# Thirteen feature units of the mixers as split products, their parts made on ScalarE and GpSimd

## The chip, the core and the metric

The kernel runs on one core of one Trainium2 chip. Five engines work side by side, each through its own list of instructions in order: TensorE (PE) multiplies, VectorE (DVE), ScalarE (ACT) and GpSimd (POOL) do the elementwise work, and SyncE (SP) issues most of the loads from device memory. They wait for one another by semaphores. The metric is the device time of the whole program in microseconds, lower is better.

## The reference

Two layers of a decoder trunk on 256 tokens of width 1024, all in float32. A layer is a half-step SwiGLU FFN (inner width 2816), a hybrid token mixer and a second FFN, each behind an RMS norm that a conditioning vector `c` shifts, scales and gates:

```python
mod = (cond @ ada_w[l] + ada_b[l]).reshape(B, N_SUBLAYERS, 3, 1, D)
h = adaln_pre(x, norm_g[l, 1], mod[:, 1, 0], mod[:, 1, 1])
p = dict(zip(names, jnp.split(h @ w_in[l] + b_in[l], splits, axis=-1)))
y_a = nsa_mixer(p["a_q"], ...)           # sparse attention
y_b = short_conv_mixer(p["b_b"], p["b_c"], p["b_x"], sc_conv_w[l])
y_c = gated_deltanet(p["c_q"], ..., p["c_z"], ...)   # chunked delta rule, triangular solve
y_d = mlstm_mixer(p["d_q"], p["d_k"], ..., p["d_o"], ...)
y = jnp.concatenate([rms_norm(y_a, ...), rms_norm(y_b, ...), y_c, y_d], axis=-1)
x = x + mod[:, 1, 2] * (y @ w_out[l])
```

The columns of `w_in` are cut into units of 128 features: `k0 k1 q0 q1 v0 v1` and `z0 z1` of the delta rule, `dq0 dq1 dk0 dk1 o0 o1` of the mLSTM, `b0 b1 c0 c1 x0 x1` of the short convolution, `aq0 aq1 ksw kvc` of the attention.

## The kernel before

Activations stand with features on the 128 partitions and the 256 tokens along them, so `h` is eight blocks of 128 × 256. A unit is a weight of 128 × 1024 and a sum over eight k-steps, one block of `h` each. There are two ways to multiply. A float32 product (`mm`) is one call and two instructions on PE. A split product (`mm3`, line 262) uses two float32r parts of each operand, the rounded value `h` and the rest `l`, and sums three products, hi·hi, hi·lo and lo·hi. `split_into` makes the parts: ACT casts, another engine subtracts. The FFNs use split products; the units of the mixer use float32 products on the whole weight and on `hF`, the float32 `h`.

In the mixer PE, DVE, ACT and POOL are switched to a written order (`InOrder`): each engine issues in the order of the source, and SP's loads go out in the order of the source too. The source is one long list, in which `step(name, n)` gives PE n k-steps of a unit, between the small products of the four head groups. Buffers come from rings of tags: `raw` has four, `wh`, `wl`, `bg` and `bx` three each. `load(tag)` takes the next unit of the list `units` and issues its load into a buffer of that tag; `used(name)`, called behind the last k-step of a unit, frees its tag and loads the next unit. While the mixer runs, `CAP` lets units use `wh` and `wl` and keeps `raw` for the adaLN weights: `ada_load` loads 128 outputs of `ada_w`, and `ada_use` is one DVE product of 128 × 1024, `aw`, with an accumulated sum.

Names that return below, in the order in which PE meets them. `lf` (DVE, from the token-major unit `td`) goes into `bc`, the cumulative sums. `glh` and `gll` are the parts of the log gates; POOL multiplies them with a triangle of `cst` into `ug`, four tiles a layer, from which PE makes the gates' differences `sg` and `sgx`. `ssc` and `rsk` are norms. `kq` and `kr` are products of the delta rule's keys and queries that DVE scales into `AP`. `MV`, `wh` and `hid` belong to the attention's compression. `nMh` and `nMl` are the parts of the mLSTM's running maxima, from which PE makes `mw`. `As`, `T`, `Q`, `Tt` and `Ab` belong to a blockwise inversion of two triangular matrices, numbered 0 and 1; POOL copies `Ab` from `As`, and PE's `q` reads it. `taps(n, u)` is a causal convolution of four taps on DVE (`cvk`, `cvq`, `cvv`), one `TENSOR_SCALAR` and three `SCALAR_TENSOR_TENSOR`. At the end the output projection takes eight units `wo`.

## Time and profile before

| | us |
|---|---|
| median of three runs | 1207.26 (1205.89 to 1207.42) |
| profiled execution | 1206.86 |
| span of its trace | 1205.1 |
| PE busy | 1176.2 (98%) |
| DVE busy | 811.3 (67%) |
| ACT busy | 473.6 (39%) |
| POOL busy | 276.6 (23%) |
| mixer of layer 0 | 228 to 424 |
| mixer of layer 1 | 810 to 1007 |

The span is what the profiler saw of one execution; the time also holds 1.8 us around it. The granted clock of PE stands at 9 tenths or more in each of the page's 40 slices. An engine's busy time counts its instructions, not its waits. In a timeline an instruction's row ends with the idle time ahead of it and with what ended that, and instructions of one kind that follow each other are one row with a count.

### The profile page before, as it was taken

What the parts mean: (1) busy time and instruction counts of PE and PEld (TensorE: products, weight loads), DVE (VectorE), ACT (ScalarE), POOL (GpSimd) and SP (SyncE); (2) the same over time, 40 slices, a digit from 0 to 9 for tenths busy, and PEclk for the clock granted to TensorE, in tenths of its full rate; (3) what the DMA queues carried; (4) which work ended last, traced back from release to release, by engine and by line L of the source; (5) the groups of instructions that cost most, each with busy time, mean ns of one, the idle gap of its engine ahead of it and who ended that gap; (6) DMA issues with size and microseconds to landing.
All of it is one profiled execution on the core that took longest, in us unless ns stands there. A gap on an engine that the chain in (4) does not pass through costs nothing.

```text
span 1205.1 us, 21205 instructions
## 1 busy us (share of the span) xinstructions
PE 1176.2 (98%) x8402; PEld 1088.6 (90%) x8402; DVE 811.3 (67%) x1536; ACT 473.6 (39%) x829; POOL 276.6 (23%) x233
## 2 busy tenths in 40 slices
PE   5999999999999999999999999999999999999998
PEld 4799999978769889999999999998776998999998
DVE  4667887258967568888647777734697774766663
ACT  3454454222222255444435444433122334544441
POOL 0022432202010033434231333220201002332321
PEclk9999999999999999999999999999999999999999
DMA  8988896466574337989756787664656442676561
GB/s 282 320 326 306 318 353 214 162 211 213 176 273 158 117 104 268 318 305 310 232 179 203 251 280 274 203 226 174 211 166 244 165 144 71 210 244 227 176 193 53
DMA packets 77748, 266.96 MB, mean 222 GB/s; under 512 B 8815, under 2 KB 14191, under 8 KB 77505
## 3 DMA queue, kind: packets, MB, share of 16 engines
q1 hardware_dynamic: 68256, 232.00, 56.1%
q0 software_dynamic: 8960, 32.88, 8.3%
q8 instruction: 66, 1.08, 0.4%
q10 hardware_dynamic: 432, 0.72, 0.2%
q14 instruction: 34, 0.28, 0.1%
HBM read 264.50 MB, written 2.24 MB: 221 GB/s over the span
## 4 chain that ended last, share of the span: by engine, by line
PE 89%; DVE 7%; DMA 2%; ACT 1%; issue 1%; ACTq 0%; SPq 0%; DVEq 0%
PE ab L198 35%; PE y L198 21%; PE e L198 8%; PE po L198 2%; PE p_td L198 2%; PE pw L198 2%; DVE aw L198 2%; PE hid L198 1%; PE p_o L198 1%; PE p_dk L198 1%; PE p_z L198 1%; PE p_aq L198 1%; PE p_x L198 1%; PE pv L198 1%; PE tq L198 1%; PE p_b L198 1%
## 5 line engine op out<-in xcount | busy, mean ns | idle before, releaser
L198 PE MATMUL y<-g,w_2h 128*128 128x256 f32 x1408 | 257.1, 284 | 0.0
L198 POOL TENSOR_TENSOR w_2l<-w,w_2h 128x1024 fp32r<-128x1024 f32 x71 | 174.7, 2461 | 355.3 <-ACT w_2h L198 314.7
L198 DVE SCALAR_TENSOR_TENSOR aw<-aw,cond 128x1024 f32<-128x1024 f32 x144 | 246.9, 1715 | 13.3 <-DMA aw<-in_adaw_dram 8.0
L198 PEld LDWEIGHTS y<-g,w_2h 128*128 128x128 f32 x1408 | 219.3, 192 | 0.9 <-issue 0.9
L198 PE MATMUL y<-g,w_2l 128*128 128x256 f32 x704 | 199.9, 284 | 0.0
L198 PE MATMUL ab<-hH,w_0h 128*128 128x256 f32 x600 | 168.9, 281 | 1.3 <-DVE sl L198 1.3
L198 PE MATMUL ab<-hH,w_1l 128*128 128x256 f32 x600 | 167.8, 280 | 1.3 <-DVE w_1l L198 1.3
L198 PE MATMUL ab<-hH,w_1h 128*128 128x256 f32 x600 | 168.2, 280 | 0.0
L198 PE MATMUL ab<-hH,w_0l 128*128 128x256 f32 x600 | 167.7, 280 | 0.0
L198 PE MATMUL ab<-hL,w_0h 128*128 128x256 f32 x600 | 167.6, 279 | 0.0
L198 PE MATMUL ab<-hL,w_1h 128*128 128x256 f32 x600 | 167.6, 279 | 0.0
L198 DVE TENSOR_TENSOR w_1l<-w,w_1h 128x1024 fp32r<-128x1024 f32 x75 | 102.7, 1369 | 57.1 <-ACT w_1h L198 56.2
L198 PEld LDWEIGHTS y<-g,w_2l 128*128 128x128 f32 x704 | 134.7, 191 | 0.0
L198 ACT CAST w_2h<-w 128x1024 fp32r<-128x1024 f32 x88 | 91.8, 1047 | 107.5 <-PE ab L198 96.7
L198 ACT CAST w_1h<-w 128x1024 fp32r<-128x1024 f32 x75 | 78.7, 1049 | 115.0 <-PE ab L198 97.9
L198 PEld LDWEIGHTS ab<-hH,w_0h 128*128 128x128 f32 x600 | 113.0, 188 | 2.1 <-issue 2.1
L198 PEld LDWEIGHTS ab<-hH,w_1l 128*128 128x128 f32 x600 | 113.0, 188 | 1.5 <-DVE w_1l L198 1.5
L198 PEld LDWEIGHTS ab<-hH,w_0l 128*128 128x128 f32 x600 | 113.0, 188 | 0.2 <-DVE w_0l L198 0.2
L198 PEld LDWEIGHTS ab<-hL,w_0h 128*128 128x128 f32 x600 | 112.8, 188 | 0.0
L198 PEld LDWEIGHTS ab<-hH,w_1h 128*128 128x128 f32 x600 | 112.7, 188 | 0.0
L198 PEld LDWEIGHTS ab<-hL,w_1h 128*128 128x128 f32 x600 | 112.4, 187 | 0.0
L198 DVE TENSOR_TENSOR sl<-sl,ab 128x256 f32<-128x256 f32 x75 | 31.5, 420 | 107.3 <-ACT sl L198 107.3
(442 smaller groups left out, 1898.8 us busy)
## 6 DMA issues: line engine op xcount, KB each, us to landing
w<-in_ffn_dram SPq DMA_DIRECT2D x238, 512.0 KB, 4.5
aw<-in_adaw_dram SPq DMA_DIRECT2D x88, 512.0 KB, 4.9
aw<-in_adaw_dram POOLq DMA_DIRECT2D x56, 512.0 KB, 5.2
we<-in_ffn_dram SPq DMA_DIRECT2D x18, 512.0 KB, 4.1
wh<-in_cw_dram SPq DMA_DIRECT2D x16, 512.0 KB, 3.6
wwo<-in_wout_dram SPq DMA_DIRECT2D x16, 512.0 KB, 3.6
we<-in_ffn_dram SPq DMA_DIRECT2D x32, 128.0 KB, 4.8
wtd<-in_wtd_dram SPq DMA_DIRECT2D x8, 412.0 KB, 4.8
```

Of the source, the lines that this page charges most:

```text
L198: r = f(*args, **kw)
```

## The change

Thirteen of the fourteen units `dq`, `b`, `c`, `x`, `dk`, `o`, `z` of each mixer become split products; b1 stays a float32 product. For each of them `ahead()`, called behind the third k-step of a running unit, takes two free buffers and issues a cast on ACT (`w…h`) and a subtraction on POOL (`w…l`), for at most two units in advance; the weight's own buffer is then free for the next load. `both(k)` makes the parts `hH` and `hL` of a block of `h`, on ACT and DVE, for four blocks between td1 and td2 and for four in front of the taps of k0. A load may now take any free buffer of `wl`, `raw` or `wh`. One load of adaLN weights of each mixer moves into the FFN ahead of it, and the whole FFN weights that are loaded early get a memset of one column or an order behind another instruction.

```diff
+        split_units = [n for n in units if n[:-1] in ("dq", "b", "c", "x", "dk", "o", "z")]
+        ready, live, firsts = {}, {}, {}
+        CAP = {"raw": 4, "wh": 3, "wl": 3, "bg": 1, "bx": 1}
+        def free(tag):
+            return CAP[tag] - list(live.values()).count(tag)
         def used(n):
-            tag = live.pop(n)
-            if units and not (tag in ("bg", "bx") or list(live.values()).count(tag) >= CAP[tag]):
-                load(tag)
+            if n in firsts:
+                live.pop(n + "h")
+                live.pop(n + "l")
+                firsts.pop(n)
+            else:
+                live.pop(n)
+            more()
+        def space():
+            return sum(max(free(t), 0) for t in ("wl", "wh", "raw"))
+        def slot():
+            return next(t for t in ("wl", "raw", "wh") if free(t) > 0)
+        def more():
+            while units and space() > (2 if split_units and len(firsts) < 2 else 0):
+                load(slot())
+        def ahead():
+            if split_units and split_units[0] in ready and len(firsts) < 2 and space() > 1:
+                n = split_units.pop(0)
+                r, both = ready[n], []
+                for c in "hl":
+                    tag = live[n + c] = slot()
+                    both.append(wk.tile([128, 1024], F32R, tag=tag, bufs=BUFS[tag], name=f"w{n}{c}"))
+                firsts[n] = ready[n] = both
+                act.copy(both[0], r)
+                pool.tensor_tensor(both[1], r, both[0].bitcast(F32), op=ALU.subtract)
+                live.pop(n)
+                more()
+        def both(k):
+            act.copy(hH[:, k], hf32(k)[:, :T])
+            dve.tensor_tensor(hL[:, k], hf32(k)[:, :T], hH[:, k].bitcast(F32), op=ALU.subtract)
@@ dense
+            if name in split_units:
+                split_units.remove(name)
                 for k in range(KD):
-                    mm(hf(p, u), w[:, 128 * k:128 * k + 128], hf32(k)[:, :T], start=(k == 0), stop=(k == KD - 1))
+                    if isinstance(w, list):
+                        mm3(hf(p, u), w, hT, (ALL, slice(128 * k, 128 * k + 128)), (ALL, k), k == 0, k == KD - 1)
+                    else:
+                        mm(hf(p, u), w[:, 128 * k:128 * k + 128], hf32(k)[:, :T], start=(k == 0), stop=(k == KD - 1))
+                    if k == 2:
+                        ahead()
@@ mixer
-        CAP["raw"] = 0
+        CAP["raw"] = 1
         step("aq1")
         placed_on_all("aq")
         ada_load(sync, "raw")
-        ada_load(sync, "raw")
...
         step("td1", 3)
+        for k in range(4):
+            both(k)
         step("td2")
...
         tanh_of("q")
+        for k in range(4, KD):
+            both(k)
         step("kvc", 2)
         taps("k", 0)
@@ calls
-        a1.run(28 if l == 0 else 20, first=(l == 0))
+        a1.run(29 if l == 0 else 21, first=(l == 0))
```

The order on POOL in the first mixer, from the first `ug` to the first copies `Ab`. Before:

```order
L198 TENSOR_TENSOR ug_2816<-cst,glh 128x512
L198 TENSOR_TENSOR ug_2818<-cst,gll 128x512
L198 MEMSET gpv 128x2x3
L198 TENSOR_TENSOR ug_2858<-cst,glh 128x512
L198 TENSOR_TENSOR ug_2860<-cst,gll 128x512
L198 MEMSET MV 128x32x16
L198 COPY Ab_3081<-As_3011 128x256
L198 COPY Ab_3135<-As_3037 128x256
```

And now, from the third subtraction on:

```order
L198 TENSOR_TENSOR wb0l<-wb_2683,wb0h 128x1024
L198 TENSOR_TENSOR ug_2883<-cst,glh 128x512
L198 TENSOR_TENSOR ug_2885<-cst,gll 128x512
L198 MEMSET gpv 128x2x3
L198 TENSOR_TENSOR wc0l<-wc_2768,wc0h 128x1024
L198 TENSOR_TENSOR ug_2937<-cst,glh 128x512
L198 TENSOR_TENSOR ug_2939<-cst,gll 128x512
L198 TENSOR_TENSOR wc1l<-wc_2822,wc1h 128x1024
L198 MEMSET MV 128x32x16
L198 TENSOR_TENSOR wx0l<-wx_2896,wx0h 128x1024
L198 TENSOR_TENSOR wx1l<-wx_2898,wx1h 128x1024
L198 TENSOR_TENSOR wdk0l<-wdk_3144,wdk0h 128x1024
```

```order
L198 TENSOR_TENSOR wdk0l<-wdk_3144,wdk0h 128x1024
L198 TENSOR_TENSOR wdk1l<-wdk_3177,wdk1h 128x1024
L198 COPY Ab_3244<-As_3128 128x256
L198 COPY Ab_3298<-As_3190 128x256
L198 COPY Ab_3376<-As_3190 128x256
```

`wc0l` stands ahead of the second pair of `ug`, which goes into `sgx`, and all subtractions up to `wdk1l` stand ahead of the first `Ab`.

The order on DVE ahead of `lf`, from the bias of the second half of the token-major values (`dvaug`) to the small tiles of the gates (`lt`). Before:

```order
L198 TENSOR_TENSOR dvaug<-p_td_2644,par_657 128x4x64
L198 SCALAR_TENSOR_TENSOR aw_46_2654,mod<-aw_46_2654,cond 128x1024
L198 TENSOR_SCALAR cvk<-gpk,par_657 128x256
L198 SCALAR_TENSOR_TENSOR cvk<-gpk,par_657,cvk 128x256 x3
L198 SCALAR_TENSOR_TENSOR aw_47_2679,mod<-aw_47_2679,cond 128x1024
L198 TENSOR_TENSOR modG<-mod,par_70 128x8
L198 TENSOR_SCALAR lt<-ex 128x16
```

And now:

```order
L198 TENSOR_TENSOR dvaug<-p_td_2643,par_657 128x4x64
L198 SCALAR_TENSOR_TENSOR aw_47_2686,mod<-aw_47_2686,cond 128x1024
L198 TENSOR_TENSOR modG<-mod,par_70 128x8
L198 TENSOR_TENSOR hL<-hF_2391,hH 128x256 x4
L198 TENSOR_SCALAR cvk<-gpk,par_657 128x256
L198 SCALAR_TENSOR_TENSOR cvk<-gpk,par_657,cvk 128x256 x3
L198 SCALAR_TENSOR_TENSOR aw_48_2714,mod<-aw_48_2714,cond 128x1024
L198 TENSOR_SCALAR lt<-ex 128x16
```

Four `hL` now stand between the two products `aw`, ahead of the taps; `lf` follows the gates' tiles in both.

The order on SP around the loads of wdk0 and wdk1, whose buffers come free as the text above says. Before:

```order
L253 DMA wx1_2803<-in_winf_dram 128x1024
L253 DMA wh0_2823<-in_cw1_dram 128x1024
L358 DMA aw0_55_3008<-in_adaw_dram 128x1024
L253 DMA wh1_2900<-in_cw1_dram 128x1024
L253 DMA wdk0_2957<-in_winf_dram 128x1024
L358 DMA aw0_56_3025<-in_adaw_dram 128x1024
L253 DMA wdk1_3005<-in_winf_dram 128x1024
```

And now:

```order
L253 DMA wx1_2898<-in_winf_dram 128x1024
L358 DMA aw0_54_3057<-in_adaw_dram 128x1024
L358 DMA aw0_55_3125<-in_adaw_dram 128x1024
L253 DMA wh0_3008<-in_cw1_dram 128x1024
L253 DMA wh1_3073<-in_cw1_dram 128x1024
L358 DMA aw0_56_3162<-in_adaw_dram 128x1024
L253 DMA wdk0_3144<-in_winf_dram 128x1024
L253 DMA wdk1_3177<-in_winf_dram 128x1024
```

The two loads of dk now follow each other; wdk0 goes into the buffer that `wx1l` releases on POOL and wdk1 into that of wdk0, released by `wdk0l`, where before the last k-step of a unit on PE released it.

## Rows read from the trace of the kernel before

**Rows 1.** Part 1 of the page.

```profile
PE 1176.2 (98%) x8402; PEld 1088.6 (90%) x8402; DVE 811.3 (67%) x1536; ACT 473.6 (39%) x829; POOL 276.6 (23%) x233
```

**Rows 2.** Windows: length, busy PE, PEld, DVE, ACT, POOL, clock, DMA share, GB/s.

```profile
228.00:424.00 196.00, 193.89 (x1100) 158.22 (x1099) 131.26 (x396) 56.02 (x146) 22.23 (x33) 1.00 0.53 178
810.00:1007.00 197.00, 195.09 (x1107) 159.35 (x1106) 132.03 (x396) 57.30 (x149) 22.70 (x33) 1.00 0.52 176
290.00:310.00 20.00, 19.33 (x101) 14.62 (x100) 17.23 (x51) 4.84 (x11) 0.55 (x1) 1.00 0.42 141
310.00:330.00 20.00, 19.60 (x121) 14.54 (x120) 17.73 (x44) 5.54 (x14) 1.81 (x4) 1.00 0.56 185
330.00:350.00 20.00, 20.00 (x126) 12.74 (x124) 13.63 (x37) 5.72 (x16) 2.58 (x5) 1.00 0.78 268
```

**Rows 3.** Timeline of PE: start, length, what, count, idle before and its releaser.

```profile
277.92 0.39 PE L198 MATMUL bc<-lf,cst 128*128 128x8 f32 x2 [0.51 <-DVE lf L198]
...
289.27 0.82 PE L198 MATMUL sg<-ug,cstR 128*128 128x512 f32 x2
...
290.59 0.63 PE L198 MATMUL sgx<-ug,onesR 128*128 128x512 f32 x2
...
307.17 6.22 PE L198 MATMUL p_x<-hF,wx 128*128 128x256 f32 x28
...
317.86 0.32 PE L198 MATMUL mw<-nMl,cstR 4*128 4x128 f32 x1 [0.40 <-DVE nMl L198]
...
320.24 0.61 PE L198 MATMUL q<-T,Ab 128*128 128x128 f32 x4
```

**Rows 4.** Timeline of DVE, same columns.

```profile
276.78 1.01 DVE L198 TENSOR_SCALAR ob<-ex 128x32 f32<-128x32 f32 x1
277.71 0.16 DVE L198 TENSOR_SCALAR lf<-sp 128x8 f32<-128x8 f32 x1
...
292.05 0.17 DVE L198 TENSOR_SCALAR xk<-ssc 128x8 f32<-128x8 f32 x1 [3.98 <-PE ssc L198]
...
309.31 1.22 DVE L198 SCALAR_TENSOR_TENSOR aw<-aw,cond 128x1024 f32<-128x1024 f32 x1
...
317.40 0.40 DVE L198 TENSOR_TENSOR nMl<-negM,nMh 4x256 fp32r<-4x256 f32 x1
```

**Rows 5.** Chain of waits: start, length, what.

```profile
69.61 5.66 PE ab L198 x48
...
249.47 6.92 PE p_aq L198 x32
```

**Rows 6.** Part 5 of the page, costliest groups of instructions.

```profile
L198 ACT CAST w_1h<-w 128x1024 fp32r<-128x1024 f32 x75 | 78.7, 1049 | 115.0 <-PE ab L198 97.9
```

**Rows 7.** Timeline in the first FFN, POOL and DVE.

```profile
99.18 2.41 POOL L198 TENSOR_TENSOR w_2l<-w,w_2h 128x1024 fp32r<-128x1024 f32 x1 [8.53 <-ACT w_2h L198]
...
99.74 2.93 DVE L198 SCALAR_TENSOR_TENSOR aw<-aw,cond 128x1024 f32<-128x1024 f32 x1
```

**Rows 8.** Groups of DVE's instructions, shapes apart.

```profile
L198 DVE TENSOR_TENSOR hL<-hF,hH 128x256 fp32r<-128x256 f32 x8 | 3.4, 423 | 1.4 <-ACT hH L198 1.4
```

**Rows 9.** Timeline of POOL in the mixer.

```profile
276.03 1.72 POOL L198 TENSOR_TENSOR ug<-cst,glh 128x512 fp32r<-128x512 f32 x1 [42.25 <-ACT glh L198]
...
283.30 1.44 POOL L198 TENSOR_TENSOR ug<-cst,glh 128x512 fp32r<-128x512 f32 x1
284.70 1.49 POOL L198 TENSOR_TENSOR ug<-cst,gll 128x512 fp32r<-128x512 f32 x1
...
309.45 1.34 POOL L198 COPY Ab<-As 128x256 f32<-128x256 f32 x1 [22.78 <-DVE As L198]
313.90 0.41 POOL L198 COPY Ab<-As 128x256 f32<-128x256 f32 x1 [3.11 <-DVE As L198]
```

**Rows 10.** DMA issues: count, KB each, median us to landing.

```profile
wdk<-in_winf_dram SPq DMA_DIRECT2D x4, 512.0 KB, 3.2
wo<-in_winf_dram SPq DMA_DIRECT2D x4, 512.0 KB, 4.5
```

## Prediction

> **What bounds the kernel now.** I read the page's busy times first: TensorE (PE) is busy 98% of 1205.1 us [rows 1], so a change must either take work off PE or make it wait. Then the windows: a mixer stretch is 196.00 us with PE busy 193.89, VectorE (DVE) 131.26, ScalarE (ACT) 56.02 and GpSimd (POOL) 22.23, and layer 1 repeats it; inside it DVE is busy 17.23 of 20 us in 290–310, 17.73 in 310–330 and 13.63 in 330–350 [rows 2]. So PE bounds the mixer as a whole, but from 290 to 330 DVE is close behind. Last I read the timelines of single engines for who ends last at each hand-over: at 277.92 PE waits 0.51 us for `lf` of DVE and at 317.86 0.40 us for `nMl` [rows 3]; `nMl` ends on DVE at 317.80 [rows 4]. At both places DVE is last already, so saved PE time ahead of them is lost, and any delay of DVE there is a delay of PE.

> **What the change saves.** A float32 k-step of a unit costs two instructions; 32 instructions took 6.92 us, so 2 × 6.92 / 32 = 0.433 us. Three split products cost 3 × 5.66 / 48 = 0.354 us [rows 5]. The difference, 0.079 us, times 8 k-steps is 0.63 us a unit; thirteen units give 8.2 us a layer, 16.4 us in all, if nothing waits.

> **What it adds off PE.** Each unit adds a cast on ACT (1.05 us) and a subtraction on POOL (2.41 us) [rows 6, 7]: 13.7 us of ACT and 31 us of POOL a layer, on engines that are idle most of the stretch. By totals it fits. The eight `hH` and `hL` halves add 8 × 0.42 = 3.4 us to DVE [rows 8]; four fall where DVE waits for `td` and cost nothing, four stand in front of the taps of k0. The load of adaLN weights that moves into the first FFN costs nothing: DVE has idle time there (67% busy over the span [rows 1]) and no queue in front of PE changes. The memsets ahead of early FFN weights are one column each; I cost them at nothing too, since nothing on DVE that PE waits for stands behind them.

> The cost is in the order. POOL, ACT, DVE and the load queue run in the written order, and a part can be made only when its slots are free. I follow layer 0, in the times of before.

> 1. *`lf` → bc.* DVE must do four `hL` (4 × 0.42 = 1.7 us) before the taps of k0. Beside them POOL subtracts `wdq1l`. In the trace a DVE operation that reads SBUF and starts under a running POOL subtraction ends only after it: POOL ran 99.18–101.59, the aw product that started at 99.74 took 2.93 us [rows 7] where it takes 1.22 alone [rows 4]. That price, up to 2.4 us, falls on the taps. Against it `ob`, 1.01 us now under POOL's first `ug`, which ran from 276.03 to 277.75 [rows 4, 9], comes free of it (about 0.17, as its neighbours on small tiles such as `lf` with 0.16): −0.84. Sum 3.3, and PE arrives 0.5 earlier (seven steps saved) and finds nothing: a wait of about 3.6. Bounds 0 and 3.8.
> 2. *b0.* Its parts need the slots of dq0's parts, free when dq0 ends on PE. From there 1.05 + 2.41 = 3.46 us, while PE has six steps of dq1, 6 × 0.354 = 2.1. Wait 1.4, with hand-overs 1.5. Bounds 1.4 and 1.8.
> 3. *sgx.* POOL's order puts `wc0l` ahead of both products `ug` of sgx. `wc0h` needs a slot that b0 frees. From b0's end: 1.05 + 2.41 + 1.44 + 1.49 [rows 9] = 6.4 us. PE has five steps of b1 (5 × 0.433) and the 1.32 us from 289.27 to 290.59 [rows 3]: 3.5. Wait 2.9, and I see no slack.
> 4. *292–307.* `wc1l` and `wx0l` run on POOL beside a full DVE, which starts here only when `ssc` arrives [rows 4] and then feeds PE at AP and kq. The 16 steps of c save 16 × 0.079 = 1.3 us that PE waits away; and each subtraction takes up to 2.93 − 1.22 = 1.7 us from DVE. I take 1.3 plus one such loss, 3.0; bounds 0 and 4.7.
> 5. *The load chain of dk.* `wx1l` needs the slot of `wc1l`, free at c1's end (PE at 307.17 before). The load of wdk0 waits for `wx1l` on POOL, that of wdk1 for `wdk0l`, and POOL's copy Ab, which PE's q at 320.24 needs [rows 3], now stands behind `wdk1l`. So: 2.41 + 3.2 (landing [rows 10]) + 1.05 + 2.41 + 3.2 + 1.05 + 2.41 + 0.41 (copy [rows 9]) = 16.1 us, with hand-overs about 16.8. Before, PE needed 320.24 − 307.17 = 13.07; less 16 steps saved in x it is 11.8. Wait 5.0. Bounds 4.3 and, with landings of 4.5 as for wo [rows 10] and ACT held up by its own casts, 8. The DVE delay from `wx1l` and `wdk0l` on `nMl` lies inside this.
> 6. *o, z.* Loads of o and z are followed by a cast and a subtraction, 3.46 us more of lead. No row shows that lead; bounds 0 (the earlier slots absorb it) and 4.5 + 1.05 + 2.41 = 8.0 for one unit whose load goes out only when it is due. PE has no idle time in 330–350 [rows 2], so little is late there now: I take one subtraction, 2.5.

> Sum a layer: 3.6 + 1.5 + 2.9 + 3.0 + 5.0 + 2.5 = 18.5, less 8.2, is +10.3; two layers +20.6. The profiled execution was 1206.86 us (span 1205.1 and 1.8 around it), the median of the runs 1207.26; from the median the forecast is 1228. All lower bounds: 0 + 1.4 + 2.9 + 0 + 4.3 + 0 = 8.6, +0.4 a layer, 1208. All upper: 3.8 + 1.8 + 2.9 + 4.7 + 8 + 8 = 29.2, +21 a layer, 1249.

> The blocking also goes the other way: POOL's copy Ab took 1.34 us at 309.45, beside an aw product of DVE that began at 309.31, and 0.41 at 313.90 [rows 4, 9]. [...]

> **Rivals.**
> *Parts in time, faster.* At b0, sgx and q the part is there when PE comes, because slots fall free and loads land earlier than I follow. The point: cast and subtraction, 3.46 us, must be shorter than PE's work between the freeing of the slot and the first use. For it: POOL is busy 22 of 196 us. Against it: steps 2, 3 and 5 are counted from an event on PE itself, so nothing earlier helps. Then 1207.3 − 16.4 = 1191; with half the saving 1199.
> *Only PE's own chains count.* DVE takes the subtractions in idle moments, and `lf` and the c steps come in time: steps 2, 3 and 5 alone, 8.6 − 8.2, so about 1208, or 1213 with step 1 at its half and some hand-overs. For it: DVE has 2 to 3 us idle in each 20. Against it: that idle time lies behind waits for PE.
> *Late loads on top.* wo0's load queues behind an aw load that waits for dk1, casts that wait for landings hold up ACT's copies, and step 5 and 6 take their upper ends: 1240 to 1249.

> **Chances.** Forecast case (1215 to 1238) 0.52; only PE's chains (1205 to 1215) 0.17, of which 0.05 within 0.2%; late loads 0.18; parts in time 0.13. A measurement of this kernel tells apart about 0.2%, 2.4 us. So faster 0.13, same 0.05, slower 0.82. The range 1204 to 1249 leaves out some 0.12 below and 0.06 above; the likeliest case alone is 1215 to 1238.

> **What would show it.** In the profile after: PE's waits in the mixer, near nothing now, name DVE `lf` (3 to 4 us before bc), POOL `wb0l` (1.5), POOL `ug` at sgx (3) and POOL Ab at q (5), in both layers; aw products beside subtractions take 2 us and more; k-steps cost 0.354. Wrong would be: a mixer under 196 us with PE still busy throughout; a wait at sgx under 1 us; Ab no longer last before q; or a difference that sits in the FFN stretches, where I expect none.

## The result, and the profile after

The changed kernel takes 1266.60 us, the median of four runs (1262.55 to 1268.46), against 1206.94 before: 1.0491 times as long, 95% interval 1.0465 to 1.0517. The direction was forecast, the size was not: 1228 stood there, with 1249 as the upper end. The profiled execution of the changed kernel was its fastest, 1262.55 us, so the account below is of the 55.7 us between it and the profiled execution of before, 1206.86.

The page's busy times and its row of the clock that TensorE was granted, one digit for each fortieth of the span:

```profile
PE 1191.2 (94%) x8610; PEld 1103.9 (88%) x8610; DVE 855.1 (68%) x1570; ACT 505.2 (40%) x871; POOL 330.5 (26%) x260
...
PEclk9899999998899999999989999999989999999999
```

TensorE was to be busy 16.4 us less; it is busy 15 us more than in [rows 1], and its share of the span falls from 98% to 94%. The second line says why both can be: in the mixers, at one place between them and in the first FFN (the second digit) it is 8, where before it was 9 throughout. The two mixer stretches in windows, with the columns of [rows 2], from the first product of the mixer to the first of the FFN behind it:

```profile
228.48:444.18 215.70, 196.87 (x1205) 162.69 (x1203) 151.87 (x408) 71.23 (x167) 49.71 (x47) 0.95 0.46 157
841.97:1061.75 219.78, 200.83 (x1209) 167.32 (x1209) 153.89 (x407) 71.92 (x169) 50.02 (x46) 0.94 0.44 154
```

Against [rows 2] the first is 19.7 us longer and the second 22.8. TensorE's idle time in them is 18.8 and 19.0 us where it was 2.1 and 1.9: 33.8 us of new waits. Its busy time is 3.0 and 5.7 us longer although its work shrank by the 8.2 us of the prediction each: that leaves 25.1 us for products at a lower clock (mean 0.95 and 0.94). So 33.8 + 25.1 − 16.4 = 42.5 us of the 55.7 lie in the mixers. TensorE's waits in the first of them, by what ended them (us in all, times, longest):

```profile
PE q L198 <- POOL Ab L198: 4.5, 2, 3.1
PE bc L198 <- DVE lf L198: 3.7, 1, 3.7
PE kq L198 <- DVE AP L198: 3.5, 1, 3.5
PE sgx L198 <- POOL ug L198: 1.7, 2, 1.2
PE hid L198 <- ACT cs L198: 1.6, 1, 1.6
PE at L198 <- DVE T L198: 1.3, 1, 1.3
PE mw L198 <- DVE nMl L198: 1.1, 1, 1.1
PE oCt L198 <- DVE no L198: 0.5, 1, 0.5
PE q L198 <- DVE T L198: 0.5, 1, 0.5
PE p_b L198 <- POOL wb0l L198: 0.2, 1, 0.2
```

And some rows of its timeline:

```profile
281.06 0.39 PE L198 MATMUL bc<-lf,cst 128*128 128x8 f32 x2 [3.73 <-DVE lf L198]
...
312.01 3.15 PE L198 MATMUL kq<-KQ 64*128 64x512 f32 x3 [3.54 <-DVE AP L198]
...
317.38 0.41 PE L198 MATMUL p_c<-hH,wc1l 128*128 128x256 f32 x1
...
319.03 0.28 PE L198 MATMUL p_c<-hL,wc1h 128*128 128x256 f32 x1
...
338.59 0.71 PE L198 MATMUL q<-T,Ab 128*128 128x128 f32 x4 [3.15 <-POOL Ab L198]
```

Behind the wait of 3.54 us a product of 128x256 takes 0.41 us, and at 319.03 the same product takes 0.28. The windows behind two of the waits (the clock is the third number from the end):

```profile
282.00:286.00 4.00, 4.00 (x23) 3.82 (x22) 3.93 (x6) 2.81 (x5) 2.35 (x1) 0.65 0.32 120
312.00:319.00 7.00, 6.99 (x22) 4.25 (x23) 6.48 (x15) 1.05 (x1) 0.00 (x0) 0.51 0.12 49
```

In the second window TensorE is busy 6.99 of 7 us at a granted clock of 0.51: 7 × 0.49, an estimate of 3.4 us lost, as much again as the wait.

Why `lf` is late, on VectorE:

```profile
270.61 3.58 DVE L198 TENSOR_TENSOR hL<-hF,hH 128x256 fp32r<-128x256 f32 x4
...
280.76 0.18 DVE L198 TENSOR_SCALAR ob<-ex 128x32 f32<-128x32 f32 x1
280.85 0.17 DVE L198 TENSOR_SCALAR lf<-sp 128x8 f32<-128x8 f32 x1
```

Four `hL` are 1.7 us of work [rows 8] and took 3.58, while POOL's `wdq1l` ran from 271.54 for 2.37 us; `ob`, 1.01 us in [rows 4], takes 0.18. `AP`, for which kq waits, is late in the same way:

```profile
301.73 0.87 DVE L198 COPY MV<-kr 64x120 f32<-64x120 f32 x4
...
302.81 3.38 DVE L198 COPY MV<-kr 64x120 f32<-64x120 f32 x4
...
307.67 2.21 DVE L198 TENSOR_SCALAR rv_t<-rv_t 128x8 f32<-128x8 f32 x1
```

Four copies took 3.38 us where the four ahead of them took 0.87, and an instruction of 128 × 8 elements 2.21 where its neighbours take 0.17; POOL's `wc1l` ran from 302.75 for 2.38 us and `wx0l` from 307.48 for 2.37. Why q is late, on POOL:

```profile
320.01 2.68 POOL L198 TENSOR_TENSOR wx1l<-wx,wx1h 128x1024 fp32r<-128x1024 f32 x1 [10.17 <-PE p_c L198]
328.88 2.41 POOL L198 TENSOR_TENSOR wdk0l<-wdk,wdk0h 128x1024 fp32r<-128x1024 f32 x1 [6.18 <-ACT wdk0h L198]
335.84 2.35 POOL L198 TENSOR_TENSOR wdk1l<-wdk,wdk1h 128x1024 fp32r<-128x1024 f32 x1 [4.55 <-ACT wdk1h L198]
338.13 0.77 POOL L198 COPY Ab<-As 128x256 f32<-128x256 f32 x2
```

The chain of loads starts at `wx1l`, released by the end of p_c on PE, and ends with the copies at 338.13, which were done at 309.45 and 313.90 in [rows 9]. The wait for `cs` (1.6 us) comes from the same chain: on ACT `cs` stands behind the cast `wdk0h`, which waited for its load until 327.75.

The third place lies between the layers. VectorE of the changed kernel, then the load queue, then TensorE:

```profile
636.88 3.23 DVE L198 SCALAR_TENSOR_TENSOR xT<-y,modG,xT 128x256 f32<-128x256 f32 x8 [4.75 <-PE y L198]
640.06 0.10 DVE L198 MEMSET we<- 128x1 f32 x6
```

```profile
640.16 2.85 SPq L615 DMA_DIRECT2D we<-in_ffn_dram  x6
```

```profile
643.68 2.49 PE L198 MATMUL e<-hF,we 128*128 128x257 f32 x4 [4.68 <-DMA we<-in_ffn_dram]
647.20 13.05 PE L198 MATMUL e<-hF,we 128*128 128x257 f32 x44 [1.03 <-DMA we<-in_ffn_dram]
```

And before, the load queue and TensorE:

```profile
595.71 1.94 SPq L253 DMA_DIRECT2D we<-in_ffn_dram  x2
...
604.62 2.48 SPq L253 DMA_DIRECT2D we<-in_ffn_dram  x4
```

```profile
617.69 10.63 PE L198 MATMUL e<-hF,we 128*128 128x257 f32 x48
```

The six early weights of FFN1 in layer 1 were loaded 11 to 22 us ahead of their first product. Now their memsets stand on VectorE behind the last eight additions into `xT`, so all six loads go out at 640.16. TensorE waits 5.7 us and then runs the same 48 products in 15.5 us in place of 10.6, 10.6 us later in all. Its granted clock in the first 7 us is 0.51:

```profile
643.00:650.00 7.00, 5.15 (x10) 2.83 (x11) 1.52 (x1) 1.09 (x2) 1.45 (x2) 0.51 0.98 387
```

### The profile page after: what moved, and what is told of

Same layout as the page of the kernel before. It is cut to its first block, busy times and chain, and to the rows that moved or that the text cites. A ratio compares the mean times of both kernels' runs of the same rounds, so it can differ in the third digit from the quotient of the medians.

```text
span 1260.8 us, 21769 instructions
## 1 busy us (share of the span) xinstructions
PE 1191.2 (94%) x8610; PEld 1103.9 (88%) x8610; DVE 855.1 (68%) x1570; ACT 505.2 (40%) x871; POOL 330.5 (26%) x260
## 3 DMA queue, kind: packets, MB, share of 16 engines
q1 hardware_dynamic: 68112, 231.47, 53.1%
## 5 line engine op out<-in xcount | busy, mean ns | idle before, releaser
L198 DVE SCALAR_TENSOR_TENSOR aw<-aw,cond 128x1024 f32<-128x1024 f32 x144 | 259.1, 1800 | 13.1 <-DMA aw<-in_adaw_dram 8.0
L198 DVE TENSOR_TENSOR w_1l<-w,w_1h 128x1024 fp32r<-128x1024 f32 x75 | 95.9, 1279 | 55.8 <-ACT w_1h L198 53.0
L198 PE MATMUL e<-hF,we 128*128 128x257 f32 (+1 forms) x416 | 103.0, 409 | 10.7 <-DMA we<-in_ffn_dram 5.7
```

The source lines that it names most:

```text
L198: r = f(*args, **kw)
```

## The experiments

**Three edits undone or done alone, and the waits filled.** In the first run FFN1's whole weights are loaded as before; in the second that edit is the only one, on the kernel before:

```diff
-                a1.whole(f, i, t, after=a2.at[8])
+                a1.whole(f, i, t)
```

> The changed kernel with one edit undone: the six whole weights of FFN1 of layer 1 are loaded without a memset ahead of them. Theory A (the memsets stand on VectorE behind the last additions into xT, so the six loads go out together at 640 us, and TensorE waits 5.7 us for them and then runs at half clock): 1255 us, 10 to 12 below the changed kernel's 1266.6, the wait of e for the weights gone and the stretch 638 to 672 back to about 21.5 us. Theory B (the twelve us at the layer boundary come from somewhere else, as from the adaLN load moved into FFN1): 1264 to 1268.

Measured 1255.62 us (1252.88 to 1261.44), 11.0 below the changed kernel.

> The kernel before with only that edit: the memsets ahead of FFN1's whole weights in layer 1. Theory A: 1217 to 1219 us, 10 to 12 above 1206.9, with the granted clock near 0.5 to 0.7 behind the wait. Theory B: 1206 to 1208.

Measured 1218.14 us, 1.0097 of before (1.0081 to 1.0113), 12.0 us. The wait of e for the weights is 6.0 us in all, and the granted clock behind it 0.50 from 620 to 627 us; the last 44 of the 48 products took 12.26 us, where all 48 took 10.63 before. Theory A holds both ways: this edit alone costs 11 to 12 us.

The third run makes all `hL` in VectorE's gap:

```diff
         step("td1", 3)
-        for k in range(4):
+        for k in range(KD):
             both(k)
...
-        for k in range(4, KD):
-            both(k)
```

> The changed kernel with all eight hL made between td1 and td2, where VectorE waits for td, instead of four there and four ahead of the taps of k0. Theory A (step 1 of the prediction: 1.7 of the 3.7 us that bc waits for lf are these four): the wait falls to about 2 us and the time by 1.7 a layer or, with the half clock behind that wait, up to 3 a layer: 1260 to 1263. Theory B (the wait is the subtraction wdq1l on GpSimd alone): wait still over 3 us, 1265 to 1268.

Measured 1259.66 us (1256.21 to 1267.38). TensorE's waits for `lf` fall from 7.4 to 4.6 us in both layers together, 1.4 each, near the 1.7 of theory A, and theory B's 3 us are not reached. What remains is the subtraction: three instructions of the taps, which begin just ahead of `wdq1l`, now take 3.70 us in place of 1.52. The time fell by 7, more than the 2.8 us of wait, but its runs spread over 11 us, so the size beyond the wait is not settled by this run.

The fourth adds products in the waits. They write into the banks of units under way, and the sums there are no longer the reference's.

```diff
+        def fill(p, n):
+            for _ in range(n):
+                mm(p, identR, zeroR.to_broadcast([128, T]), start=False, stop=False)
...
+        fill(hf(held["banks"]["dq"], 0), 28)
         p_bc = P("bc", "y")
...
+        fill(hf(held["banks"]["c"], 0), 26)
         kq(3)
```

> The changed kernel with products that add zero put where TensorE waits in both mixers: 28 of 128x256 before bc, 8 before the ug part of sgx, 26 before kq, 12 before q; they take 0.117 us each at full clock and less than the waits measured there. Theory A (behind a wait of 3 us and more TensorE is granted half clock for several us, and this lost time, some 7 us a layer, is part of the slowdown): the granted clock in 280 to 345 us stays at 1.0 and the time falls to 1250 to 1258. Theory B (the lower clock is hidden behind the waits of VectorE and GpSimd, the chain is theirs): 1265 to 1270.

Measured 1254.38 us (1248.79 to 1256.58), 1.0394 of before. With 148 products more, TensorE finishes 12 us earlier. The clock did not stay at 1.0 everywhere: it was 0.66 from 285 to 290 and 0.54 from 330 to 335 us, behind waits for `wb0l` (1.8) and `nMl` (3.4) that were short before and were not filled. So theory A holds on the time, and its clause that the clock stays at 1.0 does not: part of the gain was lost to waits that became late next. The lower clock came behind a wait of 1.8 us too.

**One wait by itself, and other ways to make the parts.** On the kernel before, `lf` is made late and nothing else:

```diff
-        taps("k", 0)
+        for _ in range(3):
+            taps("k", 0)
```

> The kernel before with the taps of k0 done three times (the same result each time), which makes lf some 3.7 us later in each mixer and nothing else. What one wait of that length costs, everything included. Theory A (the granted clock falls behind such a wait): TensorE waits about 4 us for lf twice, the granted clock falls below 1.0 in the five us behind it, and the time rises by more than the waits: 11 to 15 us, 1217 to 1221. Theory B (a wait costs its length): 1213 to 1215, granted clock 1.0.

Measured 1218.17 us, 1.0092 (1.0069 to 1.0114), 11.7 us. TensorE waited 8.6 us for `lf` in the two layers, 7.8 more than before. Its timeline and a window of the stretch behind the wait:

```profile
279.31 0.60 PE L198 MATMUL bc<-lf,cst 128*128 128x8 f32 x2 [4.40 <-DVE lf L198]
...
280.19 5.07 PE L198 MATMUL p_dq<-hF,wdq 128*128 128x256 f32 x14
```

```profile
279.00:285.00 6.00, 5.69 (x18) 4.84 (x19) 5.86 (x15) 0.63 (x1) 2.41 (x4) 0.60 0.70 222
```

The same fourteen products before:

```profile
278.39 3.27 PE L198 MATMUL p_dq<-hF,wdq 128*128 128x256 f32 x14
```

Fourteen products take 1.8 us more at a granted clock of 0.60. A wait of 4.4 us costs 3.9 us more than the 0.5 that stood there, and 2.0 again behind it. Theory A.

In the next run dk0 and dk1 stay float32 products:

```diff
-        split_units = [n for n in units if n[:-1] in ("dq", "b", "c", "x", "dk", "o", "z")]
+        split_units = [n for n in units if n[:-1] in ("dq", "b", "c", "x", "o", "z")]
```

> The changed kernel with dk0 and dk1 left float32 products. Theory A (step 5: POOL's first copy Ab stands behind wdk1l, which waits for two loads in a row): the wait of q for Ab (3.1 us in layer 0, 1.4 in layer 1 at that place) goes to 0 to 0.5, the half clock behind it too, against 1.3 us a layer of lost saving: 1258 to 1263. Theory B (q would then wait for something else, DVE's T or nMl): 1265 to 1270.

Measured 1251.07 us (1248.51 to 1252.51). No wait of q at 331 us is left, and the granted clock is 1.00 there:

```profile
330.00:335.00 5.00, 5.00 (x31) 3.29 (x31) 4.65 (x11) 3.44 (x10) 0.40 (x1) 1.00 0.46 188
335.00:340.00 5.00, 5.00 (x32) 3.82 (x31) 3.90 (x11) 0.59 (x1) 0.00 (x0) 1.00 0.62 210
```

Theory A on the cause; the time lies 7 us under its range. The waits for `nMl` fell as well, from 4.2 to 1.2 us in both layers, and the 1.6 for `cs` went. Between the two profiled executions (1262.55 and 1248.51) 9.3 us lie in the two mixers; the rest lies in stretches that the edit does not touch, 2.3 us of it ahead of the first mixer's td. There 48 products of the first FFN, from 46 us on, took 13.63 us in the changed kernel and 10.77 here; the section on why the prediction was wrong returns to this place.

With o and z alone, `hL` in the gap and no memsets for FFN1:

```diff
+        split_units = [n for n in units if n[:-1] in ("o", "z")]
```

> Only o0, o1, z0 and z1 split, all eight hL made between td1 and td2, and FFN1's whole weights loaded without memsets. The saving is 4 x 0.63 x 2 = 5.0 us. Theory A (without waits of 3 us ahead of it the clock stays up, and the waits behind wz0l and wz1l, 1.3 us each for Ab and T in the changed kernel, are all that is left): 1204 to 1208. Theory B (the subtractions of o and z also make waits that lower the clock): 1210 to 1216.

Measured 1209.50 us over ten runs, 1.0024 (1.0011 to 1.0036): slower than before by 3 us, between the two theories. Its waits are 2.6 us for Ab and 3.0 for T in both layers, as theory A named them. But the clock does not stay up, and it falls behind a wait of 1.3 us:

```profile
363.76 0.71 PE L198 MATMUL q<-T,Ab 128*128 128x128 f32 x4 [1.29 <-POOL Ab L198]
```

```profile
364.00:366.00 2.00, 2.00 (x12) 1.91 (x12) 1.73 (x9) 0.00 (x0) 0.79 (x3) 0.59 0.74 256
```

Behind it the products of 128x256 take 0.41 to 0.45 us each. In layer 1 the same wait, 1.30 us, was followed by a granted clock of 1.00, and these products take 0.28 there from the second on. How T comes late, on POOL and then on VectorE:

```profile
376.77 2.35 POOL L198 TENSOR_TENSOR wz1l<-wz,wz1h 128x1024 fp32r<-128x1024 f32 x1 [4.86 <-ACT wz1h L198]
```

```profile
377.38 1.75 DVE L198 TENSOR_TENSOR rk_t<-rk_y 15x1 f32<-15x1 f32 x1
...
379.86 0.15 DVE L198 TENSOR_TENSOR rk_t<-rk_y 15x1 f32<-15x1 f32 x1
```

A product of 15 × 1 elements takes 0.15 us alone and 1.75 under a subtraction on POOL; it ended at 379.13, the subtraction at 379.12.

> The changed kernel with the subtractions of the parts on VectorE (1.23 us alone) in place of GpSimd (2.41 us). Theory A (GpSimd's subtractions delay VectorE by their overlap and its own queue by their length): POOL's waits at sgx and q go, kq waits less, 1245 to 1258. Theory B (VectorE is full from 267 to 330 us and now waits in order for the casts): waits for lf, AP and nMl grow, 1268 to 1285.

```diff
-                pool.tensor_tensor(both[1], r, both[0].bitcast(F32), op=ALU.subtract)
+                dve.tensor_tensor(both[1], r, both[0].bitcast(F32), op=ALU.subtract)
```

Measured 1264.21 us (1263.27 to 1265.73): neither theory's range. The waits for Ab and `ug` go, but others take their place:

```profile
PE mw L198 <- DVE nMl L198: 14.0, 2, 7.1
...
PE bc L198 <- DVE lf L198: 9.2, 2, 4.7
PE kq L198 <- DVE AP L198: 6.8, 4, 1.9
```

So it is not GpSimd as such: from 267 to 330 us VectorE has no room for these subtractions either.

**Versions that could beat both.**

```diff
+        split_units = [n for n in units if n[:-1] in ("o",)]
```

> As the run with o and z split, but z0 and z1 stay float32 products. The saving is 2 x 0.63 x 2 = 2.5 us. Theory A (of the 3 us of waits a layer in that run, 1.3 for Ab behind wz0l and 1.3 to 1.7 for T under wz1l, all go with z): 1204 to 1206. Theory B (the subtractions of o slow VectorE's T too): 1206.5 to 1209.

Measured 1203.32 us over eight runs (1201.87 to 1204.77), 0.9972 of before (0.9960 to 0.9984), somewhat better than theory A. The mixers show no wait that the kernel before had not. The gain of 3.2 us is more than the 2.5 of the products, within the interval of 1.9 to 4.8. This run keeps the rest of the change, the freer choice of buffers and the moved load of adaLN weights, which was not run by itself; what that is worth alone is not shown.

```diff
-                    if k == 2:
+                    if k == {"o1": 4, "z0": 3}.get(name, 2):
                         ahead()
...
-                pool.tensor_tensor(both[1], r, both[0].bitcast(F32), op=ALU.subtract)
+                (dve if n[0] == "z" else pool).tensor_tensor(both[1], r, both[0].bitcast(F32), op=ALU.subtract)
```

> As the run with o and z split, but the two subtractions of z stand on VectorE (1.23 us), issued behind the fifth k-step of o1 and the fourth of z0, so that no copy Ab and no T stands behind them. Theory A (o and z pay as soon as their parts hold up nobody): the waits for Ab and T go, the saving of 5.0 us comes through but for some tenths, 1201 to 1204. Theory B (the subtractions delay what follows on VectorE, the scores of the compressed attention): 1206 to 1210.

In this run the calls of `ahead()` behind the products of `wo2` and `wo3` are also left out. Measured 1203.59 us over nine runs, 0.9972 (0.9961 to 0.9983). The waits for Ab and T are gone, 2.8 us a layer, and the loss of the run with o and z turns into a gain. But z's own 2.5 us do not come through beside o alone: one new wait of 0.6 us a layer for `nd` on VectorE accounts for half; the other half stays open. The time lies in theory A's range and the waits went as it says, but the saving of 5.0 us came through only to 2.9.

```diff
-                a1.whole(f, i, t, after=a2.at[8])
+                a1.whole(f, i, t)
...
-        split_units = [n for n in units if n[:-1] in ("dq", "b", "c", "x", "dk", "o", "z")]
+        split_units = [n for n in units if n[:-1] in ("dq", "b", "c", "x", "o", "z")]
```

with `hL` in the gap as above:

> The changed kernel with three edits undone together: FFN1's whole weights loaded without memsets (11 us alone), all eight hL between td1 and td2 (7 alone), dk0 and dk1 float32 (15.5 alone). If the three are separate places with their own waits and their own half clock, the sum: 1266.6 - 33.5 = 1233, within 5. If one wait is taken over by the next: 1240 to 1248.

Measured 1236.67 us (1233.05 to 1239.70), against a sum of 1233 within 5: this fits three separate places, each with its own wait.

## Why the prediction was wrong

The direction, the late parts and the sum of the waits in the mixers were right, and two steps of the sum failed.

*The waits in the mixers.* 18.5 us a layer were forecast, 18.8 and 19.0 us of idle time are there, of which 2 stood there before: 16.7 and 17.0 are new. Term by term in the first layer: `lf` 3.6 (its own terms, 3.3 and 0.5, make 3.8), measured 3.73, of which 0.51 stood there, and the price fell on `hL`, not on the taps; b0 1.5, measured 0.24, and sgx 2.9, measured 1.7, both smaller since TensorE came to them late, behind the wait for `lf` and 4 us at a granted clock of 0.65 (with the wait before bc filled, b0 waited 1.8); kq 3.0, with one loss to a subtraction, measured 3.54, of which 0.7 stood there, with two; the load chain of dk 5.0, measured 3.15 at q, with 1.6 for `cs` and 1.1 for `nMl` in the same stretch; o and z 2.5, measured 0.5 + 1.35 + 1.32. That the sum is nearer than its terms is in part luck: b0 and sgx fell short by 2.5, and the waits for `cs` and `nMl`, which have no term of their own, stood in for them. The chain of step 5 took 19.0 us from c1's end to q, 16.8 were forecast: the first load landed only 5.0 us after its issue. Its three subtractions, counted at 2.41 each, took 2.68, 2.41 and 2.35. What step 1 says of a VectorE operation under a subtraction holds for the `aw` of [rows 7] and not for every one: `sl` of 128 × 256, begun at 99.40 under the same subtraction, took 0.42 us and ended ahead of it.

*First failure: a wait was priced at its length.* The sum of the change has terms for waits and for products and none for the rate of the products behind a wait. "Wait of about 3.6" was counted as 3.6. The runs show waits of 3 to 4 us followed by 4 to 7 us at a granted clock of 0.5 to 0.65: 25.1 us in the two mixers, by the account above. That the time behind a wait is lost as well is shown by filling the waits (−12.2 us with more work) and by one wait alone (7.8 us of wait, 11.7 of time). [rows 2] do not show it: the mixers of before hold only some 2 us of idle time each, and the clock stands at 1.00 in every window. But the trace of before has such a place, in the first FFN, and the prediction did not look there:

```profile
45.99 12.23 PE L198 MATMUL e<-hF,we 128*128 128x256 f32 x48 [2.61 <-ACT hF L198]
```

```profile
46.00:50.00 4.00, 4.00 (x11) 3.29 (x12) 3.92 (x7) 1.86 (x5) 0.00 (x0) 0.59 0.93 282
```

The same place in the changed kernel, and in the run with `lf` late:

```profile
46.60 13.63 PE L198 MATMUL e<-hF,we 128*128 128x256 f32 x48 [3.21 <-ACT hF L198]
```

```profile
46.32 10.64 PE L198 MATMUL e<-hF,we 128*128 128x256 f32 x48 [3.33 <-ACT hF L198]
```

In the run with `lf` late the granted clock behind the wait is 1.00. Over the thirteen traces of this case the wait at this place is 2.3 to 4.0 us long; in ten of them the products behind it take 12.1 to 13.6 us, in three 10.6 to 10.8, and the length of the wait does not tell which. So a row for the price was there, and the price is not fixed: here it lies between nothing and 3.0 us.

*Second failure: "I cost them at nothing too, since nothing on DVE that PE waits for stands behind them".* The memsets ahead of FFN1's whole weights do not hold up VectorE; they are held up by it. What counts is what stands in front of them, the last additions into `xT`, and who waits behind them, six loads. Alone this is 11 to 12 us; in the profiled execution 5.7 are wait and 4.9 clock. It is also the sign of being wrong that the prediction named last, a difference in an FFN stretch.

Put together for the profiled executions: waits 33.8 + 5.7, clock 25.1 + 4.9, work −16.4, in all 53.1 of 55.7. The other 2.6 lie in the FFNs, in differences of 0.5 to 1.2 us a stretch, less than the runs of one kernel spread.

The saving itself is real: where the granted clock is 1.00, a k-step of three products takes 0.351 us in the trace after (33 products of p_c start between 303.38 and 307.12 us), and 0.354 was forecast. The run with o alone is faster by about its share of it. *Parts in time* failed for the reason given; *only PE's own chains count* failed, since `lf` and kq were late; *late loads on top* comes nearest by its time; a cast that waits for its load did hold up a copy of ACT (`cs`, 1.6 us), but the rest of the excess has the two causes above.

## What to carry to other kernels

## What the hardware showed

The runs of the changed kernel spread over 5.9 us and those with `hL` in the gap over 11; the kernel before spreads over 1.5 in four runs beside the changed one and over 6.5 in thirteen later ones. In the trace of the run with FFN1's loads free the first mixer is longer than in the changed kernel, 208.4 us against 201.9 up to the same place, with the same instructions and a mean clock of 0.91 against 0.95: what the clock lost behind waits at the same places differed between these two executions. The place in the first FFN says the same: 48 products took 10.64 us behind a wait of 3.33 and 12.23 behind one of 2.61. And small VectorE operations ended with a subtraction on GpSimd that ran when they began: one of 15 × 1 elements took 1.75 us and ended at 379.13, the subtraction at 379.12 (run with o and z), and one of 128 × 8 took 2.21 us and ended at 309.88, `wx0l` at 309.85 (changed kernel), where their like take 0.15 and 0.17. In these rows what a subtraction cost VectorE was the part of it still to run when the operation began, and did not follow the size of what it held up.
